# Query, key and value projection of a two-layer encoder: the input comes with tokens along the free axis, the norm's channel gains go onto the weights, its row factors behind the products

## Chip, cores and metric

One core of a Trainium2 chip runs the whole program. The metric is device time in microseconds (us) of one execution; lower is better.

## What is computed

The reference is a two-layer encoder of 1024 tokens with 1024 channels. Only its first step is touched by the change:

```python
def rmsnorm(x, gain):
    y = x32 * lax.rsqrt(jnp.mean(x32 * x32, axis=-1, keepdims=True) + EPS)
    return (y * gain.astype(jnp.float32)).astype(x.dtype)
...
    qkv = h @ w_qkv            # h = rmsnorm(x, attn_norm); w_qkv is 1024 x 1536
    q = rmsnorm(q, q_gain)     # per head of 64
    k = rmsnorm(k, k_gain)
    q = apply_axial_rope(q, cos, sin) * (HEAD_DIM ** -0.5)
    k = apply_axial_rope(k, cos, sin)
```

Behind it come attention with 16 query and 4 key/value heads, two cross-attentions, two gated feed-forward parts with a convolution, a pooling mixer and a last norm.

## The kernel before, in words

Tokens are cut into 8 tiles of 128 rows, channels into 8 blocks of 128. A float32 operand of a product is split into a high part (ScalarE, `high`, line 664) and a low part (VectorE, `low`, line 667); a product is three matmuls for each channel block (lines 745 to 747: high by high, high by low, low by high). TensorE contracts over the partition axis, so the left operand has to lie with channels on partitions.

In the first stage (`attention`, lines 758 to 1101) the normed input is got so, tile by tile, in `plan_rows(t)`: a load of 128 tokens (`scr<-in_x`), the sum of squares of each row (line 726, ScalarE), the factor 1/sqrt (lines 718 and 720, GpSimd), row times factor times gain (line 851, VectorE), eight transposes on TensorE (line 856, here called a row turn), and the split of the turned tile from PSUM into `hT`. Weights come in 11 pieces of 256 columns (`plan_weights`; K, V, a second copy of V called "late", and 8 pieces of Q), each in two loads with a split of its own. `plan_gemm` is one product of a token tile with a piece: 24 matmuls of 256 columns. A K or Q product is then normed per head, rotated, split and turned back (`plan_head`, `plan_k`, `plan_q`); the two turns of a K tile stand in line 988, that of a Q tile in line 1014. The rotation of K needs a table `tabK`, which GpSimd makes from the loaded table and the key gain (lines 820 and 827).

The list `QKV` sets the order of the products. Each step is entered in a `Plan` with a kind, a size and what it reads and writes. The plan gives every step a due time from TensorE's order and writes the instructions of each engine out in one fixed order; each engine then works through its own list and waits where its next entry isn't ready. All loads are issued from one queue (SyncE, shown as SP), also in that order. Raw loads share six buffers called `scr`.

Of the kernel before, what the change touches and what calls it, by code (L numbers as in the profile page):

```python
# [628 lines left out]
class Kernel:  # L629
# [131 lines left out]
    def attention(self):  # L761
        nc, R, a, tc = self.nc, self.R, self.a, self.tc
        w = a["attn_w_qkv"][0]
        xin = a["x"][0]
# [31 lines left out]
        with tc.tile_pool(name="qk", bufs=1, reuse_waits="tile") as qk, self.psum("psq", 1, 6) as self.ps:  # L796
# [40 lines left out]
                                 uses=["tabK"] if z == "K" else ())  # L837


            def plan_rows(t):  # L840
                h, junk, banks = ("h", t), ("hjunk", t), [("hturned", t, g) for g in range(2)]

                def fetch():
                    at[h] = self.scr()
                    nc.sync.dma_start(out=at[h], in_=xin[t * P:(t + 1) * P, :])

                def square():
                    at["r", t] = self.row_rstd(at[h])

                def norm():  # L850
                    nc.vector.scalar_tensor_tensor(at[h], at[h], at.pop(("r", t)), at["gain"], op0=OP.mult, op1=OP.mult)

                def turn():
                    at[banks[0]] = [self.psB() for _ in range(2)]
                    for b in range(NK):
                        nc.tensor.transpose(at[banks[0]][b // 4][:, b % 4 * P:(b % 4 + 1) * P], at[h][:, b * P:(b + 1) * P],
                                            self.ident)

                def part(g, j):
                    hi, lo = (R.v(s, 4)[:, :, t % 4 * P:(t % 4 + 1) * P] for s in hT[t // 4][2 * g:2 * g + 2])  # L860
                    src = at[banks[0]][g].rearrange("p (a b) -> p a b", a=4)
                    self.low(hi, lo, src) if j else self.high(hi, src)
                plan.add("load", 1, fetch, (), [h], [("scr", h)])
                plan.add("square", 1024, square, [h], [("hr", t)], [("A", junk)], [h])
# [8 lines left out]
            def plan_weights(piece, c0, s):  # L873
# [3 lines left out]
                for g in range(2):  # L877
                    raw, k = ("wraw", piece, g), ("w", s, g)

                    def fetch(raw=raw, g=g):  # L880
                        at[raw] = self.scr().rearrange("p (a b) -> p a b", a=4)
                        nc.sync.dma_start(out=at[raw], in_=src[:, 4 * g:4 * g + 4, :])

                    def high(raw=raw, g=g):
                        self.high(h[:, 4 * g:4 * g + 4], at[raw])

                    def low(raw=raw, g=g):
                        self.low(h[:, 4 * g:4 * g + 4], l[:, 4 * g:4 * g + 4], at.pop(raw))
                    plan.add("load", 1, fetch, (), [raw], [("scr", raw)])
                    plan.add("copy", 1024, high, [raw], [k], uses=[raw])  # L890
                    plan.add("add", 1024, low, [raw, k], [k], uses=[raw])


            def plan_gemm(it, piece, t, ended=lambda: None, gives=None):
                s, b = where[piece], ("out", it)
                wh, wl = (self.R_(z).rearrange("p (a b) -> p a b", a=8) for z in sets[s])

                def emit():
                    p = at[b] = self.psB()[:, :256]
                    for k in range(NK):  # L900
                        self.mm3(p, *self.blk(hT[t // 4], k, slice(t % 4 * P, (t % 4 + 1) * P)), wh[:, k], wl[:, k],
                                 k == 0, k == NK - 1)
                    ended()
                plan.add("product", 12.4, emit, [("hT", t, g) for g in range(2)] + [("w", s, g) for g in range(2)], [b],
                         [("B", b)], gives=gives)
                return b

            def plan_v(t, b):
                v = R.tiles[V[t // 4]].rearrange("p (k h c) -> p k h c", k=4, h=4)[:, t % 4]
                src = lambda: at[b].rearrange("p (h c) -> p h c", h=4)  # L910
                plan.add("copy", 360, lambda: self.high(v[:, :, :HD], src()), [b], [("V", t)], uses=[b])
                plan.add("add", 340, lambda: self.low(v[:, :, :HD], v[:, :, HD:], src()), [b, ("V", t)], [("V", t)], uses=[b])

            def plan_head(it, kind, t, b):

# [10 lines left out]
                    nc.vector.tensor_reduce(at[ss], at.pop(sq).rearrange("p (h c) -> p h c", h=4), axis=AX.X, op=OP.add)  # L926

                def rstd():
                    at[ss] = self.rstd(at[ss], 4, HD)

                def scaled():
                    at[qn] = buf("qn", 2)
# [19 lines left out]
                plan.add("scale", 2.9, rstd, [ss], [ss])  # L952
# [103 lines left out]
                plan.add("scale", 2.7, scale, [("inv", u), x], [x], late=7.0)  # L1056

            def main():
                def load_gain():
                    at["gain"] = self.bcast(a["attn_norm"][0])  # L1060
                plan.add("load", 1, load_gain, (), ["gain"], [("scr", "gain")])
                plan_rows(0)
                todo, count = [], 0
                plan_weights("K", NH * HD, 0)
                plan_tables()
                for it in QKV:
                    kind, t = it[0], it[-1]
                    if kind == "S":
                        plan_scores(t)
                        continue  # L1070
                    if kind == "V":
                        if t == 0:
                            plan_weights("V", (NH + NKV) * HD, 1)
# [1033 lines left out]
```

## Time and profile before

| | |
|---|---|
| median of 3 runs | 2520.91 us (2518.69 to 2521.32) |
| the profiled execution: first to last instruction (span) | 2515.8 us |
| median less that span | 5.1 us |
| TensorE busy in the span | 2481.4 us (99%) |
| VectorE, ScalarE, GpSimd busy | 1997.3, 1353.9, 396.6 us |
| granted TensorE clock over the span | 0.999 |

The profile gives a span for its execution and no time from outside; the 5.1 us stand for the start and the end of an execution around it. Busy shares of TensorE are rough, because matmuls overlap: the waits and the idle time in front of an instruction say more.

### The profile page before, as it was taken

Reading aid. Unit: us, or ns where it says so; the run is one execution under the profiler, and the core shown is the slowest. Engines: PE = TensorE matmul, PEld = TensorE weight load, DVE = VectorE, ACT = ScalarE, POOL = GpSimd, SP = SyncE. Lnnn points to the kernel's source line nnn. Section 1 sums busy time; section 2 is a strip of 40 time slices with the busy share of each in tenths; the row PEclk is TensorE's granted clock in tenths of the full one; section 3 lists DMA queues with packets and bytes.
Section 4 is the critical chain, followed back from the end, with each engine's and each line's share of the span. In section 5 each row is a group of like instructions: output and inputs, shape, how many; then the busy total and the mean of one; then the engine's idle time right before and its main releaser. Section 6 shows DMA issues by size and latency. Waiting matters only on the chain.

```text
span 2515.8 us, 37106 instructions
## 1 busy us (share of the span) xinstructions
PE 2481.4 (99%) x13481; PEld 2129.7 (85%) x13481; DVE 1997.3 (79%) x2946; ACT 1353.9 (54%) x2301; POOL 396.6 (16%) x532
## 2 busy tenths in 40 slices
PE   8999999999999999999999999999999999999998
PEld 7998888888899888888888888889888888887887
DVE  7879999974886379888879776887559988888875
ACT  5558888863555245554555333655436555554542
POOL 5664545531002000000000002102010000000001
PEclk9999999999999999999999999999999999999999
DMA  4200000042495133333348563388223424337852
GB/s 162 91 18 1 1 1 1 2 155 72 159 313 211 48 91 107 105 105 106 105 161 277 192 202 103 117 284 309 80 75 102 120 84 119 111 93 245 285 188 97
DMA packets 309531, 320.71 MB, mean 127 GB/s; under 512 B 13157, under 2 KB 244685, under 8 KB 309349
## 3 DMA queue, kind: packets, MB, share of 16 engines
q1 hardware_dynamic: 309349, 318.35, 38.9%
q8 instruction: 106, 1.74, 0.3%
q14 instruction: 76, 0.62, 0.1%
HBM read 230.90 MB, written 82.58 MB: 125 GB/s over the span
## 4 chain that ended last, share of the span: by engine, by line
PE 84%; DVE 7%; issue 4%; ACT 2%; DMA 1%; POOL 1%; SPq 0%; DVEq 0%; POOLq 0%; ACTq 0%
PE pB L745 22%; PE pB L747 22%; PE pB L746 22%; PE pA L747 3%; PE pA L745 3%; PE pA L746 3%; PE pA L778 2%; DVE nm L788 2%; PE pB L739 2%; PE pB L1133 1%; DVE R L667 1%; DVE PT L673 1%; PE pB L1134 1%; ACT scr L791 1%; PE pB L323 1%
## 5 line engine op out<-in xcount | busy, mean ns | idle before, releaser
L745 PE MATMUL pB<-R,R 128*128 128x512 f32 (+1 forms) x2732 | 1015.7, 372 | 7.4 <-DVE scr L439 2.3
L747 PE MATMUL pB<-R,R 128*128 128x512 f32 (+1 forms) x2728 | 1007.5, 369 | 1.3 <-DVE R L667 1.2
L746 PE MATMUL pB<-R,R 128*128 128x512 f32 (+1 forms) x2732 | 1008.3, 369 | 0.0
L745 PEld LDWEIGHTS pB<-R,R 128*128 128x128 f32 x2732 | 514.8, 188 | 99.9 <-DVE scr L439 4.4
L747 PEld LDWEIGHTS pB<-R,R 128*128 128x128 f32 x2728 | 514.0, 188 | 89.0 <-DVE R L667 2.6
L746 PEld LDWEIGHTS pB<-R,R 128*128 128x128 f32 x2732 | 515.0, 188 | 85.3 <-DVE R L673 0.3
L664 ACT ACTIVATE R<-scr 128x512 fp32r<-128x512 f32 (+2 forms) x340 | 256.9, 782 | 223.6 <-DMA scr<-Gs 61.3
L667 DVE TENSOR_TENSOR R<-scr,R 128x512 fp32r<-128x512 f32 (+2 forms) x340 | 289.8, 881 | 27.1 <-ACT R L664 26.6
L667 DVE TENSOR_TENSOR R<-X,R 128x512 fp32r<-128x512 f32 x374 | 252.0, 685 | 66.8 <-ACT R L664 66.1
L664 ACT ACTIVATE R<-X 128x512 fp32r<-128x512 f32 x374 | 231.7, 630 | 132.4 <-PE pB L746 65.5
L718 POOL TENSOR_SCALAR ms<-ss 128x1 f32<-128x1 f32 (+2 forms) x101 | 30.6, 303 | 1682.1 <-ACT R L726 1279.8
L437 ACT COPY scr<-pB 128x512 f32<-128x512 f32 x156 | 91.3, 585 | 190.2 <-PE pB L747 184.2
L794 POOL TENSOR_SCALAR scr<-scr,inv 128x1024 f32<-128x1024 f32 x125 | 141.0, 1128 | 163.0 <-DVE inv L793 161.1
L673 DVE TENSOR_TENSOR PT<-pB,PT 128x512 fp32r<-128x512 f32 x256 | 163.8, 680 | 1.7 <-ACT PT L672 0.7
L1702 DVE TENSOR_TENSOR X<-pB,X 128x512 f32<-128x512 f32 (+1 forms) x145 | 99.2, 686 | 82.5 <-PE pB L747 81.7
L791 ACT ACTIVATE scr<-pA,nm 128x1024 f32<-128x1024 f32 x125 | 139.7, 1118 | 41.3 <-DVE nm L788 40.1
L788 DVE TENSOR_REDUCE nm<-pA 128x1 f32<-128x1024 f32 x125 | 152.4, 1219 | 0.0
L745 PE MATMUL pA<-R,R 128*128 128x512 f32 (+1 forms) x420 | 150.6, 359 | 0.0
L747 PE MATMUL pA<-R,R 128*128 128x512 f32 (+1 forms) x420 | 150.3, 358 | 0.0
L746 PE MATMUL pA<-R,R 128*128 128x512 f32 (+1 forms) x420 | 149.9, 357 | 0.0
L778 PE MATMUL pA<-R,R 128*128 128x512 f32 x512 | 144.9, 405 | 0.0
L672 ACT ACTIVATE PT<-pB 128x512 fp32r<-128x512 f32 x256 | 138.9, 597 | 11.1 <-PE pB L739 10.7
(160 smaller groups left out, 3521.2 us busy)
## 6 DMA issues: line engine op xcount, KB each, us to landing
X<-in_ffn_w_up SPq DMA_DIRECT2D x82, 512.0 KB
Gs<-X SPq DMA_DIRECT2D x105, 256.0 KB
scr<-in_ffn_w_down SPq DMA_DIRECT2D x45, 512.0 KB
scr<-Gs SPq DMA_DIRECT2D x35, 512.0 KB
scr<-in_xattn_w_kv SPq DMA_DIRECT2D x32, 512.0 KB
scr<-Gs SPq DMA_DIRECT2D x42, 384.0 KB
scr<-in_attn_w_qkv SPq DMA_DIRECT2D x22, 512.0 KB
Wt<-scr SPq DMA_DIRECT2D x44, 256.0 KB
```

The lines of the kernel that those rows point to most:

```text
L664: self.nc.scalar.activation(hi, src, AF.Copy)
L667: self.nc.vector.tensor_tensor(out=lo, in0=src, in1=hi.bitcast(F32), op=OP.subtract)
L672: nc.scalar.activation(hi, src, AF.Copy)
L673: nc.vector.tensor_tensor(out=lo, in0=src, in1=hi.bitcast(F32), op=OP.subtract)
L745: mm(out, ah, bh, start=start, stop=False)
L746: mm(out, ah, bl, start=False, stop=False)
L747: mm(out, al, bh, start=False, stop=stop)
L778: nc.tensor.matmul(s[:, kh * 512:(kh + 1) * 512], q, R.v(K[part][kh], 4)[:, kv], start=part == 0, stop=part == 1)
L788: nc.vector.tensor_reduce(nm, s, axis=AX.X, op=OP.max, negate=True)
L791: nc.scalar.activation(pr, s, AF.Exp, bias=nm, accum_out=rs)
L794: nc.gpsimd.tensor_scalar(pr, pr, ri, 1.0, op0=OP.mult, op1=OP.mult)
L1702: nc.vector.tensor_tensor(out=x, in0=banks[b][:, c], in1=x, op=OP.add)
```

## The change

The host hands over two more arrays: the input transposed (`xt`, channels by tokens) and the gains as 128 x 8 (`gains`). `plan_rows` is gone. `plan_x` loads 256 tokens at once with channels on partitions and splits them straight from the load. The gain of a channel is now a factor of the weight's split (`plan_weights`, one instruction for each channel block, so 8 for each piece on ScalarE and on VectorE in place of 2). `plan_scales` still loads the rows and gets their sums of squares, and keeps for each tile the mean square, EPS times it, and the factor. The factor scales V behind its product; for Q and K it cancels in the norm per head, where EPS times the mean square takes the place of EPS.

```diff
-QKV = (("K", 0), ("V", 0), ("K", 1), ("V", 1), ("K", 2), ("V", 2), ("K", 3), ("V", 3),
+QKV = (("K", 0), ("K", 1), ("V", 0), ("V", 1), ("K", 2), ("V", 2), ("K", 3), ("V", 3),
...
+                    at["ss", t] = self.stat(1, "ss")
+                    nc.scalar.activation(self.psA(), at.pop(h), AF.Square, accum_out=at["ss", t])
+                def scales():
+                    m, e, r = (z[:, t:t + 1] for z in at["rows"])
+                    nc.gpsimd.tensor_scalar(m, at.pop(("ss", t)), 1.0 / D, EPS, op0=OP.mult, op1=OP.add)
+                    nc.gpsimd.tensor_scalar(e, m, EPS, 1.0, op0=OP.mult, op1=OP.mult)
+                    nc.gpsimd.tensor_tensor(out=r, in0=m, in1=self.mh[:, :1], op=OP.pow)
...
+            def plan_x(p, n):
+                def fetch(c):
+                    k0, w = c * 8 // n, 8 // n
+                    at["x", p, c] = self.scr()[:, :w * 256].rearrange("p (k n) -> p k n", k=w)
+                    nc.sync.dma_start(out=at["x", p, c], in_=xt[k0 * P:(k0 + w) * P, p * 256:(p + 1) * 256].rearrange(
+                        "(k p) n -> p k n", p=P))
...
-                plan.add("tap", 1024, norm, [h, ("hr", t), "gain"], [h], uses=[h, "gain"])
-                plan.add("turn", 8, turn, [h], banks, [("B", k) for k in banks], [h])
-                for g in range(2):
-                    k = ("hT", t, g)
-                    plan.add("copy", 512, partial(part, g, 0), banks[g:g + 1], [k], uses=banks[g:g + 1])
-                    plan.add("add", 512, partial(part, g, 1), [banks[g], k], [k], uses=banks[g:g + 1])
+                    plan.add("load", 2 / n, partial(fetch, c), (), [raw], [("scr", raw)])
+                    plan.add("copy", 2048 // n, partial(part, c, 0), [raw], [k], uses=[raw])
+                    plan.add("add", 2048 // n, partial(part, c, 1), [raw, k], [k], uses=[raw])
...
+                        for j, b in enumerate(ks):
+                            nc.scalar.activation(h[:, b], at[raw][:, j], AF.Copy, scale=at["gain"][:, b:b + 1])
...
+                            nc.vector.scalar_tensor_tensor(l[:, b], r[:, j], at["gain"][:, b:b + 1], h[:, b].bitcast(F32),
+                                                           op0=OP.mult, op1=OP.subtract)
...
-                plan_rows(0)
-                plan_weights("K", NH * HD, 0)
+                    nc.sync.dma_start(out=at["gain"], in_=a["gains"])
+                plan_x(0, 4)
+                plan_weights("K", NH * HD, 0, 4)
+                plan_scales(0)
+                plan_scales(1)
...
-                    if kind == "K" and t + 1 < NT:
-                        plan_rows(t + 1)
+                    if kind == "K" and t % 2 == 0 and t + 2 < NT:
+                        plan_x(t // 2 + 1, 2)
+                        plan_scales(t + 2)
+                        plan_scales(t + 3)
```

The SP queue's new list begins: the gains; four loads of K weights and four of `xt`, each of 256 KB; two of V weights; the rows of token tile 0; the rotation table; the two head gains; the rows of tile 1; two loads of `xt` for tokens 256 to 511; from there on all are of 512 KB.

ScalarE's list at its start, before (T_100 is the high part of the K weights, R_77 and R_79 that of the left operand; DMAHW, DVE and PE in the brackets are what an entry waits for):

```order
L726 ACT_TABLE_LOAD
L726 ACTIVATE pA,ss<-scr 128x1024 [waits DMAHW0_49]
L664 ACTIVATE T_100<-scr 128x1024 [waits DMAHW2_49]
L664 ACTIVATE T_100<-scr 128x1024 [waits DMAHW3_49]
L664 ACTIVATE R_77<-pB 128x4x128 [waits PE_49]
L664 ACTIVATE R_79<-pB 128x4x128 [waits PE_49]
```

and in the change, where DMAHW1 is the first load of K weights and DMAHW0 that of the gains:

```order
L896 ACT_TABLE_LOAD [waits DMAHW1_49]
L896 ACTIVATE T_100<-scr,gain 128x256 [waits DMAHW0_49]
L896 ACTIVATE T_100<-scr,gain 128x256
L896 ACTIVATE T_100<-scr,gain 128x256 [waits DMAHW2_49]
L896 ACTIVATE T_100<-scr,gain 128x256
L896 ACTIVATE T_100<-scr,gain 128x256 [waits DMAHW3_49]
L896 ACTIVATE T_100<-scr,gain 128x256
L896 ACTIVATE T_100<-scr,gain 128x256 [waits DMAHW4_49]
L896 ACTIVATE T_100<-scr,gain 128x256
L664 ACTIVATE R_77<-scr 128x2x256 [waits DMAHW5_49]
```

The table load stood free at the head and now stands behind a wait; eight weight splits stand ahead of the first split of the input.

VectorE's list from the first product's sum of squares to the split K tile, in the change (qn is the normed head, rb its rotated part, R_78 and R_80 the low part of the left operand, R_85 the split K tile):

```order
L944 TENSOR_REDUCE ss_238<-sq 128x4 [waits Activation_49]
L944 TENSOR_REDUCE ss_269<-sq 128x4 [waits Activation_49]
L954 TENSOR_TENSOR qn<-pB,rs 128x256 [waits Pool_49]
L667 TENSOR_TENSOR R_78<-scr,R_77 128x4x256 [waits DMAHW0_49,Activation_49]
L667 TENSOR_TENSOR R_80<-scr,R_79 128x4x256 [waits DMAHW1_49,Activation_49]
L962 TENSOR_TENSOR rb<-qn,scr 128x8x16 [waits DVE_49,Pool_49]
L962 TENSOR_TENSOR rb<-qn,scr 128x8x16 [waits Pool_49]
L966 TENSOR_TENSOR qn<-qn,scr 128x256 [waits DVE_49]
```

The low parts of the next 256 tokens now stand behind the first head's `qn`, which waits for GpSimd, and ahead of its rotation. TensorE's list where the first turn of a K tile comes (L1009; L988 before), as a piece of the difference:

```order
 L746 MATMUL pB<-T_101,R_79 128x256
 L747 MATMUL pB<-T_100,R_80 128x256
-L856 MATMUL pB<-ident,scr 128x128 x8
+L1009 MATMUL pB<-ident,R_85 128x128 x8
 L745 MATMUL pB<-R_73,R_77 128x256
 L746 MATMUL pB<-R_74,R_77 128x256
```

A row turn is gone there, and the first K turn follows the fifth product, as it did before. From the first attention product on, the lists of all engines are the same in both kernels.

## Rows read from the trace of the kernel before

**Rows 1.** The page: span, TensorE's share, and the chain that ended last.
```profile
span 2515.8 us, 37106 instructions
...
PE 84%; DVE 7%; issue 4%; ACT 2%; DMA 1%; POOL 1%; SPq 0%; DVEq 0%; POOLq 0%; ACTq 0%
```

**Rows 2.** Waits of TensorE from 0 to 180 us: in total, times, longest.
```profile
PE pB L856 <- DVE scr L851: 8.0, 1, 8.0
PE pB L747 <- DVE R L667: 2.5, 2, 2.0
PE pB L745 <- ACT R L664: 1.2, 1, 1.2
```

**Rows 3.** Timeline at the start: start us, us, engine, line, operation, tiles.
```profile
0.71 1.28 ACT L726 ACT_TABLE_LOAD   x1 [0.71 <-PEq L2089]
0.72 0.39 SPq L845 DMA_DIRECT2D scr<-in_x  x1
...
4.34 1.03 ACT L726 ACTIVATE pA<-scr 128x1024 f32<-128x1024 f32 x1 [2.34 <-DMA scr<-in_x]
...
11.14 0.58 PE L745 MATMUL pB<-T,R 128*128 128x256 f32 x1 [1.21 <-ACT R L664]
```

**Rows 4.** Busy time by stretch: length, engines, granted clock, DMA share, GB/s.
```profile
0.00:2.00 2.00, 0.00 (x0) 0.00 (x0) 0.07 (x1) 1.28 (x1) 0.69 (x6) 1.00 0.13 16
2.00:16.00 14.00, 6.25 (x29) 5.55 (x30) 7.37 (x8) 7.28 (x10) 1.51 (x4) 1.00 1.02 328
```

**Rows 5.** Timeline, TensorE: pace of the products, the first K turn.
```profile
15.03 0.41 PE L746 MATMUL pB<-T,R 128*128 128x256 f32 x1
15.24 0.33 PE L747 MATMUL pB<-T,R 128*128 128x256 f32 x1
15.41 0.28 PE L745 MATMUL pB<-T,R 128*128 128x256 f32 x1
15.53 0.28 PE L746 MATMUL pB<-T,R 128*128 128x256 f32 x1
...
33.52 1.06 PE L988 MATMUL pB<-ident,R 128*128 128x128 f32 x8 [0.66 <-DVE R L973]
```

**Rows 6.** Chain that ended last, a row turn of it: start us, us.
```profile
40.29 0.87 PE pB L856 x8
```

**Rows 7.** Groups by shape, 0 to 180 us: busy us, mean ns.
```profile
L667 DVE TENSOR_TENSOR R<-scr,R 128x1024 fp32r<-128x1024 f32 x12 | 14.2, 1218 | 0.0
L667 DVE TENSOR_TENSOR qst<-qn,qst 128x256 fp32r<-128x256 f32 x32 | 13.6, 426 | 7.5 <-ACT qst L664 7.4
L664 ACT ACTIVATE qst<-qn 128x256 fp32r<-128x256 f32 x32 | 13.3, 415 | 3.5 <-POOL qn L949 3.4
L851 DVE SCALAR_TENSOR_TENSOR scr<-scr,rs 128x1024 f32<-128x1024 f32 x8 | 11.5, 1433 | 7.7 <-DMA scr<-in_attn_norm 5.8 <-POOL rs L720 1.9
L664 ACT ACTIVATE R<-pB 128x512 fp32r<-128x512 f32 x16 | 9.0, 593 | 1.9 <-PE pB L856 1.8
```

**Rows 8.** Timeline: the first K tile's chain, on GpSimd, ScalarE and VectorE.
```profile
19.11 1.29 POOL L820 TENSOR_TENSOR scr<-tab,gk 128x512 f32<-128x512 f32 x1 [5.58 <-DVE R L667]
20.49 0.19 POOL L718 TENSOR_SCALAR ms<-ss 128x1 f32<-128x1 f32 x1
21.28 1.87 POOL L827 TENSOR_TENSOR scr<-tab,gk 128x128 f32<-128x128 f32 x2
23.52 1.02 POOL L720 TENSOR_TENSOR rs<-ms,mh 128x4 f32<-128x4 f32 x1
26.71 1.46 DVE L945 TENSOR_TENSOR qn<-qn,scr 128x256 f32<-128x256 f32 x1
31.52 0.73 POOL L949 TENSOR_TENSOR qn<-qn,rb 128x256 f32<-128x256 f32 x1
32.29 0.63 ACT L969 ACTIVATE R<-qn 128x512 fp32r<-128x512 f32 x1 [6.49 <-POOL qn L949]
```

**Rows 9.** Busy time by stretch, as rows 4: the stage's later part.
```profile
50.00:175.00 125.00, 125.00 (x1066) 124.78 (x1065) 104.70 (x247) 64.90 (x130) 87.48 (x109) 1.00 0.21 64
```

More of the change, by code (lines that the diff above doesn't have):

```diff
@@ L763, in attention @@
         w = a["attn_w_qkv"][0]
-        xin = a["x"][0]
+        xin, xt = a["x"][0], a["xt"]
         K = [[R.get() for _ in range(2)] for _ in range(2)]
@@ L837, in plan_tables, with plan_scales @@
                                  uses=["tabK"] if z == "K" else ())
-            def plan_rows(t):
-                h, junk, banks = ("h", t), ("hjunk", t), [("hturned", t, g) for g in range(2)]
+            def plan_scales(t):
+                h, junk = ("h", t), ("hjunk", t)
                 def fetch():
@@ L847, in square @@
                 def square():
[L848 to L857, printed above, removed]
@@ L859, in part @@
-                def part(g, j):
-                    hi, lo = (R.v(s, 4)[:, :, t % 4 * P:(t % 4 + 1) * P] for s in hT[t // 4][2 * g:2 * g + 2])
-                    src = at[banks[0]][g].rearrange("p (a b) -> p a b", a=4)
-                    self.low(hi, lo, src) if j else self.high(hi, src)
-                plan.add("load", 1, fetch, (), [h], [("scr", h)])
-                plan.add("square", 1024, square, [h], [("hr", t)], [("A", junk)], [h])
-                plan.add("tap", 1024, norm, [h, ("hr", t), "gain"], [h], uses=[h, "gain"])
@@ new lines, in scales @@
+                def scales():
[3 more added lines that the diff above has]
+                    nc.gpsimd.tensor_tensor(out=r, in0=m, in1=self.mh[:, :1], op=OP.pow)
+                plan.add("load", 1, fetch, (), [h], [("scr", h)])
+                plan.add("square", 1024, square, [h], [("hss", t)], [("A", junk)], [h])
@@ new lines, in plan_scales, with part @@
+                plan.add("scale", 2.8, scales, [("hss", t)], [("hr", t)])
+            def plan_x(p, n):
[4 more added lines that the diff above has]
+                        "(k p) n -> p k n", p=P))
+                def part(c, j):
+                    k0, w = c * 8 // n, 8 // n
+                    hi, lo = (R.v(s, 4)[:, k0 % 4:k0 % 4 + w, p % 2 * 256:p % 2 * 256 + 256]
+                              for s in hT[p // 2][k0 // 4 * 2:k0 // 4 * 2 + 2])
+                    src = at["x", p, c]
+                    self.low(hi, lo, src) if j else self.high(hi, src)
+                for c in range(n):
+                    raw, k = ("xraw", p, c), ("hT", p, c * 4 // n, c)
+                    at["xkeys"].setdefault(p, []).append(k)
+                    plan.add("load", 2 / n, partial(fetch, c), (), [raw], [("scr", raw)])
+                    plan.add("copy", 2048 // n, partial(part, c, 0), [raw], [k], uses=[raw])
+                    plan.add("add", 2048 // n, partial(part, c, 1), [raw, k], [k], uses=[raw])
@@ L874, in plan_weights @@
+            def plan_weights(piece, c0, s, n=2):
                 where[piece] = s
@@ L876, in plan_weights, with fetch, high, low @@
                 h, l = (self.R_(z).rearrange("p (a b) -> p a b", a=8) for z in sets[s])
[L877 to L891, printed above, removed]
+                for g in range(n):
+                    raw, k, ks = ("wraw", piece, g), ("w", s, g * 2 // n), range(g * 8 // n, (g + 1) * 8 // n)
+                    def fetch(raw=raw, ks=ks):
+                        at[raw] = self.scr()[:, :256 * len(ks)].rearrange("p (a b) -> p a b", b=256)
+                        nc.sync.dma_start(out=at[raw], in_=src[:, ks[0]:ks[-1] + 1, :])
+                    def high(raw=raw, ks=ks):
+                        for j, b in enumerate(ks):
+                            nc.scalar.activation(h[:, b], at[raw][:, j], AF.Copy, scale=at["gain"][:, b:b + 1])
+                    def low(raw=raw, ks=ks):
+                        r = at.pop(raw)
+                        for j, b in enumerate(ks):
+                            nc.vector.scalar_tensor_tensor(l[:, b], r[:, j], at["gain"][:, b:b + 1], h[:, b].bitcast(F32),
+                                                           op0=OP.mult, op1=OP.subtract)
+                    plan.add("load", 2 / n, fetch, (), [raw], [("scr", raw)])
+                    plan.add("copy", 3200 // n, high, [raw, "gain"], [k], uses=[raw])
+                    plan.add("add", 3200 // n, low, [raw, k, "gain"], [k], uses=[raw])
             def plan_gemm(it, piece, t, ended=lambda: None, gives=None):
@@ L903, in emit @@
                     ended()
-                plan.add("product", 12.4, emit, [("hT", t, g) for g in range(2)] + [("w", s, g) for g in range(2)], [b],
+                plan.add("product", 12.4, emit, at["xkeys"][t // 2] + [("w", s, g) for g in range(2)], [b],
                          [("B", b)], gives=gives)
@@ L909, in plan_v, with low @@
                 v = R.tiles[V[t // 4]].rearrange("p (k h c) -> p k h c", k=4, h=4)[:, t % 4]
-                src = lambda: at[b].rearrange("p (h c) -> p h c", h=4)
-                plan.add("copy", 360, lambda: self.high(v[:, :, :HD], src()), [b], [("V", t)], uses=[b])
-                plan.add("add", 340, lambda: self.low(v[:, :, :HD], v[:, :, HD:], src()), [b, ("V", t)], [("V", t)], uses=[b])
+                src, r = lambda: at[b].rearrange("p (h c) -> p h c", h=4), at["rows"][2][:, t:t + 1]
+                def low():
+                    nc.vector.scalar_tensor_tensor(v[:, :, HD:], src(), r, v[:, :, :HD].bitcast(F32), op0=OP.mult, op1=OP.subtract)
+                plan.add("copy", 360, lambda: nc.scalar.activation(v[:, :, :HD], src(), AF.Copy, scale=r), [b, ("hr", t)], [("V", t)],
+                         uses=[b])
+                plan.add("add", 350, low, [b, ("V", t)], [("V", t)], uses=[b])
             def plan_head(it, kind, t, b):
@@ L928, in rstd @@
                 def rstd():
-                    at[ss] = self.rstd(at[ss], 4, HD)
+                    ms, rs = self.stat(4, "ms"), self.stat(4, "rs")
+                    nc.gpsimd.tensor_scalar(ms, at[ss], 1.0 / HD, at["rows"][1][:, t:t + 1], op0=OP.mult, op1=OP.add)
+                    nc.gpsimd.tensor_tensor(out=rs, in0=ms, in1=self.mh[:, :4], op=OP.pow)
+                    at[ss] = rs
                 def scaled():
@@ L951, in plan_head @@
                 plan.add("add", 340, reduce, [sq], [ss], uses=[sq])
-                plan.add("scale", 2.9, rstd, [ss], [ss])
+                plan.add("scale", 2.9, rstd, [ss, ("hr", t)], [ss])
                 plan.add("add", 340, scaled, [b, ss], [qn], [("qn", qn)], [b])
@@ L1058, in main @@
             def main():
+                at["gain"] = self.cst.tile([P, NK], F32, name="gain")
+                at["rows"] = [self.cst.tile([P, NT], F32, name=f"rows{j}") for j in range(3)]
+                at["xkeys"] = {}
                 def load_gain():
-                    at["gain"] = self.bcast(a["attn_norm"][0])
-                plan.add("load", 1, load_gain, (), ["gain"], [("scr", "gain")])
-                plan_rows(0)
+                    nc.sync.dma_start(out=at["gain"], in_=a["gains"])
+                plan.add("load", 0.1, load_gain, (), ["gain"], late=-30.0)
+                plan_x(0, 4)
+                plan_weights("K", NH * HD, 0, 4)
                 todo, count = [], 0
-                plan_weights("K", NH * HD, 0)
+                plan_scales(0)
+                plan_scales(1)
                 plan_tables()
@@ L2101 @@
     arrays = {n: np.ascontiguousarray(inputs[n]) for n in _INS}
+    arrays["xt"] = np.ascontiguousarray(inputs["x"][0].T)
+    arrays["gains"] = np.ascontiguousarray(inputs["attn_norm"][0].reshape(NK, P).T)
     arrays["rope"] = rope_tables()
```

1 line of the change is left out of this document (removed).

## The prediction

> **What bounds the kernel now.** The page comes first: TensorE holds 84% of the chain that ended last [rows 1]. So an edit pays where TensorE stands still, or does work that can go. In the first stage both are there. The table of waits puts TensorE's idle time up to 180 us at 8.0 us ahead of the first row turn, 2.5 and 1.2 us inside the first products [rows 2], and 0.66 us ahead of the first turn of a K tile at 33.52 us [rows 5]. Behind that point it waits for nothing: from 50 to 175 us it is busy all 125 us, VectorE 104.7, GpSimd 87.5, ScalarE 64.9 [rows 9]. The second thing to see is a row turn, 0.87 us on the chain [rows 6]; there are eight, four ahead of 33.52 us and four behind it. So I need two numbers: when the first K turn starts in the changed kernel, and what TensorE saves behind it. The lists of all engines agree from the first attention product on, so what is won in this stage should move everything behind it as a block.
>
> **The start.** Nothing of the rows, factors or row turns is ahead of the first product any more; it needs the first split of the K weights and of the input. Loads move nearly nothing up to 2 us and then 0.328 MB per us [rows 4]. The first load of 0.52 MB would have its last byte at 3.6 us, and ScalarE began on it at 4.34 [rows 3], so 0.75 us more goes by until an engine starts. In the change the first 0.26 MB of weights are thus there at 2.0 + 0.8 + 0.75 = 3.55 us. The activation table's load, 1.28 us, was free at 0.71 us [rows 3]; now it stands behind that wait: 4.85 us. Eight weight splits of 256 columns follow; the nearest row is 0.415 us for one on ScalarE [rows 7], less some overlap of neighbours, so 8 x 0.37 = 3.0 us (0.415 at most, 3.3 us): 7.85 us. The first part of the input has landed before (1.31 MB: 2.0 + 4.0 + 0.75 = 6.75 us), its high part takes 0.59 us [rows 7], and the first product starts at 8.4 us instead of 11.14 [rows 3]. The gains are 4 KB in tiny pieces, an operation the trace doesn't have; between nothing and the first weights' own landing they cost nothing, and each us beyond that would cost one here.
>
> TensorE's granted clock is 1.00 in the stretches [rows 4], but the pace is that of the 1.2 GHz level up to 15.24 us, 0.21 us for 256 columns, and then 0.12 [rows 5], after TensorE had begun at 8.0 us. K0 and K1 are 48 matmuls: all at the slow pace 10.1 us, with 7.2 us of it, as before, 7.2 + 14 x 0.12 = 8.9 us, so they end near 17.3 us. V0 and V1, 24 x 0.12 = 2.85 us each, end at 23.0 (their weights: 3.1 MB, 2.0 + 9.6 + 0.75 = 12.4 us, and some 3.5 us of splits, so 16). K2 needs the second 256 tokens; it can start at 23.0, meets their low part at about 23.6 (below), and ends near 26.3 us.
>
> **The first K turn.** It follows K2, and it hangs on a chain that does not touch TensorE. The key gain is the load behind 4.25 MB: 2.0 + 13.0 + 0.75, and 0.7 us in which the queue runs dry, because the third load of the input takes the buffer of the first weights and can only be issued at about 6 us: 16.4 us. Then, in GpSimd's order: the cosine table 1.3, three small operations of the row factors 1.1 (two took 20.49 to 21.28, the third is the added one), two sine parts 1.9, the head's mean square and power 0.3 + 1.0 [rows 8]: 22.0 us. VectorE makes `qn` (0.35, a bit under the 0.426 of that shape, by overlap), and now the two low parts of the next 256 tokens stand ahead of the rotation, 2 x 1.2 [rows 7]: 24.75. Before, such a low part read PSUM and stood elsewhere. Their loads (5.8 MB: 21.2 us) are there by 22.4 with the high part, so the wait is for the order, not for the data. Rotation, three operations of 0.43: 26.0; GpSimd's sum 0.73: 26.8; ScalarE's high part 0.63: 27.4 [rows 8]; VectorE's low part 0.43: 27.85; the turn at 28.0 us. TensorE has stood still for 28.0 - 26.3 = 1.7 us there, and 0.6 us within K2. Against 33.52 us this is 5.5 us earlier. The bounds: if the chain is quicker than I think, TensorE's own work sets 26.4 us (7.1 us earlier); if all loads of the front land 3 us later, 31.0 us (2.5 us earlier).
>
> **Behind it.** The same products and turns remain, less four row turns: 4 x 0.87 = 3.5 us [rows 6]. That holds if the others keep up. VectorE loses eight norms, 11.5 us [rows 7], and gets 9 pieces of weights after K and V with eight operations of 0.39 us (0.426 less overlap) in place of two of 1.2: 0.7 us each, 6.5 us; the low parts of the input cost about the same from a load as from PSUM. Its idle time of 20.3 us in 125 [rows 9] covers that; without cover each us would be one. ScalarE gets 9 x (8 x 0.37 - 2 x 1.03, by the nearest row of that length [rows 3]) = 8 us and has 60 idle. GpSimd gets one small operation for each tile, under 0.3 us, and has 37 idle. Four MB more of loads are spread over 60 us at a DMA share of 0.21 [rows 9]; a late one would hold up ScalarE's list, with the K products behind it. I take zero for all of these, and keep 0 to 3 us for the range.
>
> The sum, against the profile's own time: 5.5 + 3.5 = 9.0 us of the 2515.8 us span [rows 1], and the same off the median, which is 5.1 us above that span: 2520.9 - 9.0 = 2511.9 us.
>
> **Rivals.** (a) *The front wins nothing.* The K chain hangs on loads and GpSimd, and 2 MB more stand in the queue ahead of the tables' first use. If the key gain lands at 21.9 instead of 16.4 us, the K turn is at 33.5 again, and only the row turns count: 2520.9 - 3.5 = 2517.4. For it: the chain has no slack by my sum. Against: 0.328 MB per us is the mean of 14 us with a DMA share of 1.02 [rows 4], and before, GpSimd waited for a VectorE release and not for the tables [rows 8]. (b) *Slower, by GpSimd and VectorE in each other's way.* The 72 small weight operations read two operands from SBUF. One VectorE operation of that size took 1.46 us instead of 0.43 [rows 8]. If each of the 72 waited 0.5 us, half a power on GpSimd [rows 8], that is 36 us, less 20.3 - 6.5 = 13.8 us of idle time: 22 us on TensorE's wait for `qn` and for banks, so 2520.9 - 9.0 + 22 = 2534. It ends above 2520.9 from 0.32 us for each ((13.8 + 9.0)/72). Against: the 32 low parts of Q of the same shape, with both operands in SBUF, took 0.426 us in the mean [rows 7], so the usual wait is near zero. The Trainium skill, "SBUF — State Buffer", section "Who interferes with whom", states that a VectorE instruction with two SBUF inputs and a GpSimd one that reads SBUF exclude each other, and the later blocks. By that rule the added operations are the wrong kind, and moving the low part of the input from PSUM to SBUF is too; the trace agrees in the one row of 1.46 us, and by its mean of 0.426 us it happens seldom. (c) *The stage behind takes no notice*: 2520.9, if the attention's start hung on something else than the last products. The lists there are the same and TensorE doesn't wait from 50 to 175 us [rows 9], so this is nearly out, and so is that the change doesn't do what it says: the row turns are gone from TensorE's list.
>
> **How the numbers follow.** Forecast 0.72, its own range 2508 to 2515.8; (a) 0.18, 2515.8 to 2519; (b) 0.07; (c) 0.03. A measurement of this kernel can tell about 0.2%, 5 us, from no change. Faster by more: the forecast and little else, 0.72. Within 0.2%: (a), (c), 0.21. Slower: 0.07. The range runs from 2508 (the K turn at 26.4 us and a quicker clock at the start, 12.9 us in all) to 2518 (two thirds of (a)), which leaves out (b), (c), the end of (a) and a little below: under 2 in 10.
>
> **What would show it.** First product at 8.0 to 9.0 us, with the table load behind the first weights; the key gain's table operation at 16 to 17.5 us; two low parts of the input between `qn` and the rotation; the first K turn at 26.5 to 30 us with a wait of 1 to 3 us; no wait of TensorE above 0.5 us from 35 to 165 us; the first attention product some 9 us earlier. I am wrong if the K turn comes after 31 us, if TensorE waits for weights or the input in the middle of the stage, or if operations of 256 columns on VectorE average above 0.6 us.

## The result, and the profile after

The changed kernel is slower: 2525.11 us, median of 10 runs, against 2519.38 us of 10 runs of the kernel before in the same session; the ratio is 1.0024, 95% interval 1.0014 to 1.0033. Medians are of all executions, ratios leave out those far above the rest (6420.48 us here, 3090.16 and 5057.42 us of before_lag below). Forecast were 2511.9 us, 2508 to 2518.

The page after, the lines that answer to [rows 1]:

```profile
span 2522.8 us, 37131 instructions
...
PE 88%; DVE 4%; issue 3%; ACT 2%; POOL 2%; DMA 1%; SPq 0%; POOLq 0%; DVEq 0%; ACTq 0%
```

TensorE sets the end even more than before, so the question is again where it stands still. Its waits up to 200 us (total, times, longest), as [rows 2]:

```profile
PE pB L745 <- ACT R L664: 9.8, 2, 9.2
PE pB L1035 <- DVE qst L667: 7.4, 10, 1.5
PE pB L747 <- DVE R L667: 2.2, 1, 2.2
PE pB L739 <- ACT R L1041: 1.9, 1, 1.9
PE pB L1009 <- DVE R L994: 1.8, 1, 1.8
```

The second line is new: ten waits of the turns of Q tiles (L1035) for the low part that VectorE makes of them. Before there was none. Stretches after, columns as [rows 4]; the second line answers to [rows 9]:

```profile
26.00:30.00 4.00, 3.87 (x21) 3.87 (x22) 2.30 (x5) 1.52 (x4) 3.56 (x6) 0.61 0.65 195
50.00:175.00 125.00, 117.59 (x987) 115.46 (x985) 102.74 (x275) 69.37 (x166) 81.17 (x109) 1.00 0.22 65
190.00:194.00 4.00, 3.67 (x15) 3.21 (x16) 1.96 (x4) 1.38 (x3) 0.00 (x0) 0.59 0.01 4
```

TensorE is busy 117.59 of 125 us instead of all of them, and VectorE is less busy than before (102.74 against 104.7): taken over the whole stretch it didn't run out of time.

The loss in three places, by the starts of the same instruction in both traces:

| | before | after | moved by | forecast |
|---|---|---|---|---|
| first K turn | 33.52 | 32.32 | -1.2 | -5.5 |
| first attention product | 170.45 | 175.59 | +5.1 | -9.0 |
| seventeenth score matmul | 186.99 | 194.56 | +7.6 | -9.0 |

From there on the two run in parallel, and the spans differ by 7.0 us (2515.8 and 2522.8). A trace is one execution, though, and executions differ: a span lay 0 to 4.3 us from its run's median, and in every trace below but that of the change the distance to the trace before grows by 1.4 to 4.8 us behind 200 us, where the lists are the same (c1 is 4.7 us ahead at 200 us and 0.5 us at its end). So verdicts go by the medians, places in the first stage by the traces; the shift at 200 us and the shift of the median agree within 2.3 us in every run. The 5.1 us given above for the start and the end of an execution hold such a difference too: in every execution on record the time was 1.7 to 2.2 us above its span.

### The profile page after: what moved, and what is told of

Same layout as the page of the kernel before. It is cut to its first block, busy times and chain, and to the rows that moved or that the text cites. A ratio compares the mean times of both kernels' runs of the same rounds, so it can differ in the third digit from the quotient of the medians.

```text
span 2522.8 us, 37131 instructions
## 1 busy us (share of the span) xinstructions
PE 2479.2 (98%) x13417; PEld 2125.4 (84%) x13417; DVE 1998.3 (79%) x2998; ACT 1367.8 (54%) x2361; POOL 397.2 (16%) x540
## 4 chain that ended last, share of the span: by engine, by line
PE 88%; DVE 4%; issue 3%; ACT 2%; POOL 2%; DMA 1%; SPq 0%; POOLq 0%; DVEq 0%; ACTq 0%
PE pB L745 21%; PE pB L747 21%; PE pB L746 21%; PE pA L778 5%; PE pB L739 4%; PE pA L747 3%; PE pA L745 3%; PE pA L746 3%; PE pB L1162 3%; PE pB L1163 2%; DVE R L667 1%; PE pB L323 1%; ACT R L664 1%; DVE R L901 1%; POOL rs L949 1%
## 5 line engine op out<-in xcount | busy, mean ns | idle before, releaser
L664 ACT ACTIVATE R<-X 128x512 fp32r<-128x512 f32 x374 | 231.6, 630 | 134.6 <-PE pB L746 65.1
L718 POOL TENSOR_SCALAR ms<-ss 128x1 f32<-128x1 f32 (+1 forms) x53 | 15.4, 291 | 1652.2 <-ACT R L726 1279.0
L672 ACT ACTIVATE PT<-pB 128x512 fp32r<-128x512 f32 x256 | 138.9, 596 | 13.0 <-PE pB L739 10.3
```

The costliest lines, as they stand in the source:

```text
L664: self.nc.scalar.activation(hi, src, AF.Copy)
L672: nc.scalar.activation(hi, src, AF.Copy)
```

## Experiments

All results first; each ratio is to runs of the kernel before on the same chip. "Q waits" are TensorE's waits for Q's low part up to 200 us, in us (and times); K turn and attention are the starts of the first K turn and of the first attention product in the profiled execution. In w2_both, w2_dve and w2_plan the gain is left out of what is computed. Runs with the same lists at the start (gain_x, c1, c3) have K turns up to 1.1 us apart, so smaller differences there say nothing.

| run | median us | less that of before | ratio, 95% interval | Q waits | K turn | attention |
|---|---|---|---|---|---|---|
| before | 2519.4 | 0 | 1 | 0 | 33.52 | 170.45 |
| the change | 2525.1 | +5.7 | 1.0024 (1.0014-1.0033) | 7.4 (10) | 32.32 | 175.59 |
| w2_both | 2521.8 | +2.5 | 1.0010 (1.0001-1.0019) | 1.9 (5) | 32.70 | 170.74 |
| w2_dve | 2527.3 | +8.0 | 1.0033 (1.0020-1.0045) | 6.5 (6) | 32.10 | 174.73 |
| w2_act | 2522.4 | +3.1 | 1.0012 (1.0003-1.0021) | 2.8 (4) | 32.43 | 171.97 |
| w2_plan | 2523.1 | +4.3 | 1.0017 (1.0008-1.0026) | 2.0 (7) | 31.83 | 172.76 |
| before_w8 | 2528.3 | +9.0 | 1.0036 (1.0024-1.0048) | 3.6 (11) | 33.54 | 177.29 |
| before_a8 | 2523.0 | +3.5 | 1.0013 (1.0004-1.0022) | 1.4 (5) | 33.84 | 173.15 |
| gk | 2524.5 | +5.7 | 1.0021 (1.0012-1.0031) | 6.2 (9) | 32.74 | 175.85 |
| xsize | 2526.0 | +6.5 | 1.0029 (1.0018-1.0040) | 7.9 (10) | 30.01 | 175.70 |
| lag5 | 2520.7 | +1.9 | 1.0007 (0.9998-1.0016) | 2.9 (5) | 30.12 | 169.11 |
| w8_lag | 2522.6 | +3.4 | 1.0015 (1.0006-1.0023) | 1.1 (4) | 33.03 | 172.84 |
| before_lag | 2520.7 | +1.4 | 1.0006 (0.9997-1.0016) | 0 | 32.47 | 169.07 |
| after_lag | 2522.7 | +3.4 | 1.0015 (1.0006-1.0024) | 3.7 (4) | 33.02 | 171.70 |
| gain_x | 2517.8 | -1.0 | 0.9996 (0.9987-1.0005) | 1.9 (7) | 28.33 | 167.20 |
| c1 | 2515.1 | -4.5 | 0.9985 (0.9976-0.9994) | 0 | 29.42 | 164.06 |
| c2 | 2517.4 | -2.1 | 0.9994 (0.9985-1.0002) | 0 | 30.14 | 165.61 |
| c3 | 2516.2 | -3.0 | 0.9992 (0.9983-1.0001) | 1.5 (2) | 29.16 | 166.23 |

### The weights' split in eight instructions

```diff
-for j, b in enumerate(ks):
-    nc.scalar.activation(h[:, b], at[raw][:, j], AF.Copy, scale=at["gain"][:, b:b + 1])
+self.high(h[:, ks[0]:ks[-1] + 1], at[raw])      # w2_both, w2_act
-for j, b in enumerate(ks):
-    nc.vector.scalar_tensor_tensor(l[:, b], r[:, j], at["gain"][:, b:b + 1], ...)
+self.low(h[:, ks[0]:ks[-1] + 1], l[:, ks[0]:ks[-1] + 1], r)      # w2_both, w2_dve
```

w2_both: 

> The changed kernel with each weight piece split by two instructions of 1024 columns on ScalarE and on VectorE, as before, in place of eight of 256; the gain is left out of the weights, order and loads stay. Theory: the ten waits of TensorE for the low part of Q (7.4 us in sum, 9.6 us with the overlap lost at each) come from the longer blocks of weight splits (VectorE 3.3 to 3.8 us instead of 2.35, ScalarE 3.4 instead of 2.1) inside a chain from product to Q turn that has no slack. Then those waits are gone and the time is about 2515 to 2517 us, 8 to 10 us below the change. Rival (the changed order and the changed loads put the waits there, not the price of the splits): the time stays at 2524 to 2526 us and the waits stay. Rival (GpSimd and VectorE exclude each other because the input's low parts now read two operands from SBUF): at most a fifth of the loss comes back, 2523 us or more.

w2_dve: 

> As the run with both engines, but only VectorE's low parts go back to two instructions for each piece (the gain is left out of the low part, ScalarE keeps its eight with the gain). If VectorE's blocks make the waits, the first wait of each pair goes (3.4 to 4 us) and the second, behind ScalarE's block, stays: about 2520.5 us. If VectorE's throughput is the limit, nearly all comes back: 2516 us. If only ScalarE's blocks matter: 2525 us.

w2_act: 

> The other half: only ScalarE's high parts go back to two instructions (the gain is left out of the high part, VectorE keeps its eight with the gain). If a block on either engine inside the chain makes a wait of its own, the second wait of each pair goes (about 4 to 5 us): 2520.5 us. If VectorE's throughput is the limit, nothing or little comes back: 2524 to 2525 us.

before_w8 (the opposite edit in the kernel before, with a column of ones): 

> The kernel before with one thing of the change alone: each weight piece is split by eight instructions for each engine with a factor from a column of ones; input, norm, loads and order stay as before. Theory of the longer blocks: ten or so waits of TensorE for the low part of Q appear, 6 to 12 us, and the time is 2526 to 2531 us; the start moves by under 1 us. Rival of the changed order: nothing appears in the middle, 2519 to 2521 us.

before_a8 (the same on ScalarE alone): 

> The kernel before, where only ScalarE's high part of the weights is made by eight instructions; VectorE keeps its two. With eight on both engines the kernel before lost 9 us. If ScalarE's block is what lengthens the chain: 2525 to 2529 us. If each engine's block costs its share: about 2523 to 2524 us. If VectorE's alone: 2519 to 2520 us.

The waits at the same turns, in before_w8 and in w2_both:

```profile
PE pB L1018 <- DVE qst L667: 3.6, 11, 0.6
...
PE pB L1032 <- DVE qst L667: 1.9, 5, 0.5
```

Where the split is the only edit, the time comes out as the theory says: 9 us more in the kernel before, 3.5 with ScalarE's alone. Of the 9 us, 6.8 stand between K turn and attention: 3.6 are the eleven new waits, where 6 to 12 were expected, some 1.8 the overlap lost at them (0.16 us each, as shown in the account of the prediction), the rest smaller pieces. In the change, two instructions on both engines take away 5.5 of 7.4 us of waits and 3.2 us of the median, less than the 8 to 10 expected. From K turn to attention it is 138.0 us instead of 143.3, where the forecast was 133.4. So the eight instructions explain 5.2 us of the 9.8 that were lost there; 4.6 us stay, some 3 of them again at Q turns, and which other part of the change brings them (the new order, the loads, the input's low parts) no run here separates.

The shares of the engines don't add up, and both halves missed their forecasts of about 2520.5 us: in the kernel before VectorE's share seems the larger, in the change w2_dve (2527.3) is no better than the change (the intervals overlap) and w2_act (2522.4) nearly as good as w2_both.

How a block makes a wait, in the timeline of the change:

```profile
110.96 3.70 DVE L901 SCALAR_TENSOR_TENSOR T<-scr,gain,T 128x256 fp32r<-128x256 f32 x8
...
114.58 0.41 DVE L667 TENSOR_TENSOR qst<-qn,qst 128x256 fp32r<-128x256 f32 x1
...
115.14 0.63 PE L1035 MATMUL pB<-ident,qst 128*128 128x128 f32 x4 [0.86 <-DVE qst L667]
...
114.64 1.70 ACT L896 ACTIVATE R<-scr,gain 128x256 fp32r<-128x256 f32 x4
116.71 1.71 ACT L896 ACTIVATE R<-scr,gain 128x256 fp32r<-128x256 f32 x4
118.33 0.40 ACT L664 ACTIVATE qst<-qn 128x256 fp32r<-128x256 f32 x1
118.76 0.86 DVE L667 TENSOR_TENSOR qst<-qn,qst 128x256 fp32r<-128x256 f32 x1 [0.99 <-ACT qst L664]
...
119.76 0.63 PE L1035 MATMUL pB<-ident,qst 128*128 128x128 f32 x4 [1.20 <-DVE qst L667]
```

and in the timeline before, at nearly the same time:

```profile
110.90 2.84 DVE L667 TENSOR_TENSOR T<-scr,T 128x1024 fp32r<-128x1024 f32 x2
113.67 0.41 DVE L667 TENSOR_TENSOR qst<-qn,qst 128x256 fp32r<-128x256 f32 x1
...
114.39 0.60 PE L1014 MATMUL pB<-ident,qst 128*128 128x128 f32 x4
...
115.52 1.06 ACT L664 ACTIVATE R<-scr 128x1024 fp32r<-128x1024 f32 x1
116.47 0.41 ACT L664 ACTIVATE qst<-qn 128x256 fp32r<-128x256 f32 x1
```

Before, the low part is ready at 113.67 + 0.41 = 114.08 us, 0.31 us ahead of its turn. The place is a typical one: over the 21 Q turns from 104 to 171 us before, the low part is ready 0.21 to 1.31 us ahead. After, the weight block ahead of it is 0.86 us longer, and TensorE waits 0.86 us (that the two numbers are equal is chance). A moment later it is ScalarE that holds up Q's high part, and with it the low part; the turn waits 1.20 us. Here the order differs too: before, one ScalarE block of 1.06 us stands ahead of that high part and the other behind it, in the change both do, 1.70 and 1.71 us, because the plan's size for a piece is larger (w2_plan, with the smaller size, has a block on either side again). That fits w2_act, which gains so much more than w2_dve; it isn't shown, as no run has eight instructions at the smaller size with the rest of the change. Turns stand four products, some 13 us, behind their own product, and the chain through ScalarE, VectorE and GpSimd takes nearly all of that.

### The plan's size for a piece

```diff
-plan.add("copy", 3200 // n, high, ...)
+plan.add("copy", 2048 // n, high, ...)
```

(and the same for `low`, on w2_both.) 

> As the run with two instructions for each piece on both engines (gain left out of the weights), and the plan's size for a piece is set back to what two instructions take (2048 in place of 3200), which moves some splits and squares in the lists of ScalarE and VectorE. If the waits that were left in that run (1.9 us, with the lost overlap 3.9 us) come from splits placed for the longer size, they go and the time is 2517 to 2519 us. If they come from the chain's phase with the shorter stage, the time stays at 2521 to 2522 us.

The waits stayed as they were (2.0 us in seven), so with two instructions the bigger size was not what put them there. The time, 2523.1 us, is above both forecasts.

### The first K turn

The rows of the change at the start, in order of time:

```profile
4.04 1.28 ACT L896 ACT_TABLE_LOAD   x1 [4.04 <-DMA scr<-in_attn_w_qkv]
9.20 0.58 PE L745 MATMUL pB<-T,R 128*128 128x256 f32 x1 [9.20 <-ACT R L664]
19.70 1.29 POOL L820 TENSOR_TENSOR scr<-tab,gk 128x512 f32<-128x512 f32 x1 [18.41 <-DMA gk<-in_attn_k_gain]
24.52 0.43 DVE L954 TENSOR_TENSOR qn<-pB,rs 128x256 f32<-128x256 f32 x1 [5.73 <-POOL rs L949]
24.86 2.61 DVE L667 TENSOR_TENSOR R<-scr,R 128x1024 fp32r<-128x1024 f32 x2
26.48 1.05 POOL L853 TENSOR_SCALAR rows<-ss 128x1 f32<-128x1 f32 x1
27.91 0.42 DVE L966 TENSOR_TENSOR qn<-qn,scr 128x256 f32<-128x256 f32 x1
29.20 1.01 POOL L949 TENSOR_TENSOR rs<-ms,mh 128x4 f32<-128x4 f32 x1
30.40 0.72 POOL L970 TENSOR_TENSOR qn<-qn,rb 128x256 f32<-128x256 f32 x1
32.32 1.09 PE L1009 MATMUL pB<-ident,R 128*128 128x128 f32 x8 [1.79 <-DVE R L994]
```

The key gain is late (19.70 us), the two low parts of the input stand between norm and rotation as forecast, and the rotation, done at 28.33, waits until 30.40 for its sum on GpSimd, which first makes the row factors of a tile and the second head's power.

gk loads the table and the head gains ahead of the V weights (`load` cut in two, with due times of its own):

> The changed kernel with the rotation table and the two head gains loaded ahead of the V weights in place of behind them; nothing else is altered. If the late key gain (its table operation at 19.70 us) holds the first K turn, the table operation starts near 14 us, the factor of the first head near 20 in place of 23.5, and the first K turn comes at 28.5 to 30 us in place of 32.3: 2 to 4 us less in all, 2521 to 2523 us; the waits for Q's low part stay. If the second 256 tokens of the input hold it (their high part at 22.3 and 23.8 us), the K turn stays at 31.5 us or later and the time at 2524 to 2526 us.

The table operation came at 15.82 us and the turn at 32.74. The V weights now landed later: ScalarE split them from 17.14 us on (13.31 in the change) and reached the squares of the rows at 20.35, and GpSimd had the table of Q in front of the row factors, which began at 21.82; VectorE had V's low part to make ahead of the head's sums. So `qn` came at 24.75. Hurrying one load only traded it for another.

xsize alters the plan's size of the input's split:

```diff
-plan.add("copy", 2048 // n, partial(part, c, 0), ...)
+plan.add("copy", 3200 // n, partial(part, c, 0), ...)
```

> The changed kernel with one number altered: the plan's size of a split of the transposed input (3200 in place of 2048), so that these splits are due earlier; the instructions are the same. In VectorE's list the two low parts of the next 256 tokens now stand ahead of the first head's norm, in GpSimd's list the first head's sum stands ahead of the second head's power. In two runs where the first norm ran at the same time (24.03 and 24.10 us), the first K turn came at 31.83 us with the lists of the change and at 28.33 us with this order. Theory (the order at the start, not the late key gain, holds the first K turn): 28 to 29.5 us here in place of 32.32, TensorE's clock not lowered around 28 us, and 3 to 5 us less in all: 2520 to 2522 us, with the waits for Q's low part as in the change. Rival (GpSimd and the loads hold it anyway): turn after 31 us, 2524 to 2526 us.

The order does hold the turn, if for less than forecast: 30.01 us with the same instructions. But the time didn't fall. In xsize's trace TensorE waited there 2.98 us in one piece, and in the stretch behind it the granted clock was 0.57:

```profile
30.01 1.77 PE L1009 MATMUL pB<-ident,R 128*128 128x128 f32 x8 [2.98 <-DVE R L994]
...
30.00:34.00 4.00, 3.99 (x21) 3.99 (x22) 3.52 (x7) 1.68 (x3) 3.75 (x6) 0.57 0.27 93
```

so the product behind it took 4.1 us in place of 3.1, and 10 Q waits were there as in the change (7.9 us); at the start of attention nothing is left of the 2.3 us. This execution, 2529.87 us, was the slowest of seven, 3.9 us above their median: whether the clock fell in the others isn't known.

### More distance, and the gains on the input

lag5 sets `LAG`, the number of products by which a turn stands behind its own, to 5 instead of 4 in the change. 

> The changed kernel with one number altered: every turn of a K or Q tile stands five products behind its own product in place of four, which gives the chain from product to turn 3.3 us more. If the waits of TensorE for the low part of Q are latency (a chain of four products' length with a longer block in it), they go: 9.6 us of waits and lost overlap and the 1.8 us ahead of the first K turn, some of it given back where the last Q turn ends the stage (up to 3.3 us): 2514 to 2518 us, against 2525. If ScalarE or VectorE can't keep the pace of the products (throughput), the waits come back a product later and the time stays within 2 us of 2525.

```diff
-                    todo.append((count + LAG, after))
+                    todo.append((count + LAG + (14 <= count < 44), after))
```

is w8_lag on before_w8: 

> The kernel before with eight instructions for each weight piece on both engines (9 us slower than before), and with turns of the tiles from the 14th to the 43rd product five products behind in place of four. Latency: the eleven waits for Q's low part go and 6 to 7 of the 9 us with them: 2520 to 2522 us; what is left is the longer split ahead of the first product. Throughput: the waits stay, 2526 to 2529 us.

before_lag, on the kernel before: 

> Control: the kernel before with nothing but that longer distance. It has no waits there to lose, so 2518 to 2521 us, and up to 1 us more at the stage's end. Were it 2515 us, the faster run would owe its gain to the distance and not to the change.

after_lag, on the change: 

> The changed kernel with nothing but that longer distance. Latency: nearly all of the ten waits go (9.6 us with the lost overlap): 2515.5 to 2518 us. Throughput: 2522 us or more, with waits of over 3 us left.

The distance brings nothing where there is no wait (before_lag), and gives back 5.6 of the 9 us that eight instructions cost the kernel before (w8_lag), with the same splits: latency, for the larger part. On the change it gives back 2.3 us (after_lag) or 3.9 (lag5) and leaves 3.7 or 2.9 us of waits. By its own forecast after_lag came out on the side of throughput, and lag5 between the two. Neither engine was full: in after_lag VectorE was busy 98.7 and ScalarE 66.9 of the 115 us from 50 to 165. Whether the chain needs yet more distance, or a stretch of it is short of an engine's time, these runs leave open.

gain_x puts the gain on the split of the input, in 32 instructions for each engine in place of 88; the plan's sizes go with it, 3200 for the input (as in xsize) and 2048 for a weight piece (as in w2_plan):

```diff
-                    self.low(hi, lo, src) if j else self.high(hi, src)
+                    for i in range(w):
+                        s = at["gain"][:, k0 + i:k0 + i + 1]
+                        if j:
+                            nc.vector.scalar_tensor_tensor(lo[:, i], src[:, i], s, hi[:, i].bitcast(F32), op0=OP.mult, op1=OP.subtract)
+                        else:
+                            nc.scalar.activation(hi[:, i], src[:, i], AF.Copy, scale=s)
```

> The channel gains on the split of the transposed input (32 blocks of 256 columns on each engine, all in the first 60 us) in place of the weights (88 blocks); each weight piece is again split by two instructions, and the plan has the sizes for that. Everything is computed. Theory of the longer blocks: the waits for Q's low part fall from 7.4 us to those of the run with two instructions on both engines (1.9 us) or less, 2519 to 2522 us; where the first K turn comes is as in the change or up to 2 us later. If order or the input's low parts make the waits: 2524 us or more.

Each against its own runs of the kernel before, gain_x is 6.7 us below the change and level with the kernel before. Attention starts 8.4 us earlier than in the change; 4.0 of that are there at the first K turn (28.33 us), where the order is that of xsize. The Q waits, 1.9 us, are those of w2_plan, which has no gain at all (2.0). c1, c2 and c3 add the distance:

> The run with the gains on the input, and in it the turns of tiles made from the 14th to the 43rd product stand five products behind, the others four. If what is left there of the waits for Q's low part (1.9 us in seven, 3.6 us with the lost overlap) is latency, it goes, at no price at the end, where the last turns keep their place: 2513 to 2515 us, below both kernels. If longer distance only moves the waits: 2517 to 2519 us.

> The run with the gains on the input, with all turns five products behind. The first K turns wait less and the Q turns not at all, but the last Q turn comes a product later, with a wait at the stage's end of up to 2 us more: 2514 to 2518 us.

> The run with the gains on the input and the longer distance, which now ends at the 35th product in place of the 43rd. If the last turns' distance is what lengthened the wait at the stage's end (1.71 and 0.38 us in place of 1.13), they fall back and the time is 2514 to 2515 us; if waits come back among the last Q turns: 2516 us.

In c1 TensorE is busy from 50 to 170 us without a gap, with VectorE at 100.89 of 120:

```profile
50.00:170.00 120.00, 120.00 (x1019) 119.63 (x1019) 100.89 (x235) 63.38 (x126) 92.90 (x113) 1.00 0.21 66
```

and it is faster than the kernel before by 0.15% (0.06% to 0.24%). c3's gain at the stage's end was paid for by two new Q waits; c1, c2, c3 and gain_x are not told apart by their intervals. What sets c1 apart is its trace: no Q wait, and 134.6 us from K turn to attention against 138.9 in gain_x.

## Why the prediction was wrong, step by step

- **First product**, 8.4 forecast, 9.20 measured: right in kind (the table load stands behind the first weights, at 4.04 us), 0.8 us small: 0.5 because the weights landed at 4.04 and not 3.55, 0.3 because the eight splits took 3.30 us and not 3.0.
- **First K turn**, 5.5 us earlier forecast, 1.2 measured: mis-sized by 4.3 us. `qn` was to come at 22.0 and came at 24.52, because the key gain's operation began at 19.70 instead of 16.4. The sum was to start at 26.0 and began at 30.40: I had counted what stands ahead of the first power in GpSimd's list, but not what stands between that power and the sum. L853, 0.23 us in the median of its eight, took 1.05 us there (26.48 to 27.53), while VectorE made low parts from two SBUF operands (24.86 to 27.47). The Trainium skill, "SBUF — State Buffer", "Who interferes with whom", states that a VectorE instruction with two SBUF inputs and a GpSimd one that reads SBUF exclude each other; this row agrees. The wait of 1.79 us ahead of the turn matches the 1.7 forecast by luck: K2 ended at 30.5 us instead of 26.3, after 2.8 us of waits ahead of it and inside it and at a lowered clock.
- **Row turns**, 3.5 us: c1 bears it out. From first K turn to first attention product it takes 134.6 us against 136.9 before, with about 1 us lost to a lowered clock and one Q turn (0.36 us) moved behind that point; before, the four row turns took 3.4 us there.
- **The step that failed**: "Its idle time of 20.3 us in 125 [rows 9] covers that", and with it the zero for ScalarE. The idle time was not slack. VectorE stood idle inside a chain of 13 us which had 0.21 to 1.31 us to spare, and the added work comes in blocks (here 3.70 us for 2.84, on ScalarE 1.70 and 1.71 us for one of 1.06 ahead of Q's high part), each of which lies in that chain. The ten waits are 7.4 us; each also loses the 0.16 us by which an undisturbed turn begins ahead of its product's modelled end: 9.0 us. From K turn to attention I forecast -3.5 us and got +6.3; 0.8 us of that difference I can't place. That the blocks make such waits is shown by before_w8; of the change's own 9.8 us they account for 5.2 (w2_both), and the cause of the other 4.6 stays open.
- **The stage behind takes the gain over as a block**: it took 2.4 us more. The turns of the first attention output wait 1.94 us instead of 1.15 for the last Q copy (L1041), and the granted clock was 0.59 in the 4 us behind. gk has the same wait with the clock at 1.00, and its stage took 0.9 us more: so about 0.9 us is the wait and 1.5 the clock. That I hadn't thought of.
- **Rivals.** It ended slower, but not by (b): the weight operations took 512 ns in the mean on VectorE, 86 ns above the 426 ns of [rows 7], where 0.32 us was the point from which it decides:

```profile
L901 DVE SCALAR_TENSOR_TENSOR R<-scr,gain,R 128x256 fp32r<-128x256 f32 x48 | 21.3, 512 | 1.8 <-ACT R L896 1.8
L896 ACT ACTIVATE R<-scr,gain 128x256 fp32r<-128x256 f32 x48 | 20.3, 498 | 2.4 <-DMA scr<-in_attn_w_qkv 2.4
```

  (a), the front wins little, came true in part (1.2 us of 5.5). None of my rivals was a wait for Q's low part. Of the signs that I named for being wrong, the K turn after 31 us came true; weights and input were not waited for in the middle of the stage.

The misses are 4.3, 9.0 + 0.8 and 2.4 us, 16.5 in all, less 0.5 by which the spans differ less than the seventeenth score matmul: the 16.0 us between -9.0 and the +7.0 of the spans. By the medians (+5.7) the miss is 14.7 us.

## What to carry to other kernels

An engine's idle share covers added work only where the engine isn't a link of a chain with a fixed distance: look for the time by which the last link is ready ahead of its user (here 0.21 to 1.31 us), and compare what a block grows by with that, not the sum with the idle time. A factor that can go on either operand belongs, by these runs, on the one with fewer split instructions (32 here, not 88): there it added no wait. When work joins such a chain, the distance has to be set anew: with the gains on the input it took away the last Q waits, and the median went from 1.0 to 4.5 us below the kernel before (the intervals overlap); in the kernel before it was worth nothing.

## What the runs showed of the hardware

The granted clock fell to about its lower level (1.2 of 2.4 GHz) right behind some waits of TensorE and not behind others: 0.61 from 26 to 30 us of the change, behind a wait of 2.23 us, and 0.57 in xsize behind 2.98 us, but 1.00 before, behind 1.95 us, and 1.00 in c3, behind 2.94 us. c1, with the same list there as c3, waited 2.07 us and had 0.50 from 30 to 32 us. At the start of attention the wait was 1.94 us in the change, in xsize and in gk; the clock in the 4 us behind was 0.59 in the first two and 1.00 in gk. Behind the first K turn (xsize, c1, gk, w2_plan) a fall cost about 1 to 1.8 us (the next product of 24 matmuls took 4.1 to 4.9 us for 3.1). What decides it, these runs don't show; the length of the wait alone doesn't.
